# A fast causal convolution on one core: three x loads move from the set-up into the blocks of the loop

## The chip, the cores and the metric

The kernel runs on 1 core of one Trainium2 chip. The metric is device microseconds of one execution; the median of three runs is given, and for profiled executions the span from the first to the last instruction. Engines are called PE (TensorE matmul), PEld (its weight load), DVE (VectorE), ACT (ScalarE), POOL (GpSimd) and SP (SyncE).

## The reference

x has shape 8 x 4096 x 512, the kernel 8 x 512 x 512, both float32. Each output row is a sum over eight taps of an earlier row times a 512 x 512 matrix; rows ahead of the sequence's start are zero.

```python
for k in range(K):                       # K = 8
    shifted = x if k == 0 else zeros in front, x[:, :-k, :]
    out += np.matmul(shifted, kernel[k])
```

## The kernel before, in words

**Tiling.** Each of the 8 sequences is cut into 16 pieces of 256 rows, which gives 128 pieces, one for each partition. Row t then means row t of all 128 pieces: a 128 x 512 matrix. The first four rows are computed directly in the set-up, tap by tap (`direct`). The other 252 are computed in 21 blocks (0 to 20) of 12 rows, block m from row t = 4 + 12 m.

**The fast algorithm.** A block isn't computed as 12 x 8 products of a row and a tap's matrix, but by a scheme that forms sums and differences of rows (on DVE) and of tap matrices (in the set-up, `wsum` and `plus`) and so needs 36 products. Each product is four matmuls of 128x128 by 128x512 (`product`, L123), added up in PSUM. A block has four nodes: PL, MI, H1, H0, in this order, numbered from 1 on: node 4m+1 is block m's PL, node 4m+3 its H1, node 4m+4 its H0. In each node DVE makes `z`, `s`, `A` and `F` (sums of transposed rows), PE multiplies them (`a1`, `a0`, `u`, `v0`, `v1`, `l00` to `l11`), ACT copies partial sums from one PSUM bank to others (the seeds `s0`, `s1`, and `dt`, a copy into the tile DT), DVE subtracts (`d0`, `d1`), and the results are combined in y tiles of float32 and stored (`e0`, `e1`, `ga`, `gb`, `ya0`). LO and HI are a node's two halves. PSUM is three pairs of banks for results (`pp0` to `pp2`) that the nodes take in turn, and a fourth for the `a` products.

**y tiles.** There are five buffers (L45), taken in turn, for cc[LO], cc[HI], dd[LO], dd[HI], yy[LO] and yy[HI] of each block. Whoever writes a new tile has to wait until the store of the tile that had its buffer five tiles ago has landed. In block 0, the H1 node's `e1` (L269) writes yy[HI] into the buffer whose last tile was cc[LO], stored by `middle` (L295). In the loop, the same `e1` writes into the buffer of the block's own cc[LO]. That tile is finished by POOL in two halves, `ga0` and `gb0` (L300), and then stored.

**How x gets in.** Except for the first rows, x takes two steps. `load_x(t)` (L106) issues a DMA from POOL's queue that reads rows t to t+3 as float32, casts them to bfloat16 and writes them to a DRAM tile xd. Each xd tile has a buffer of its own. `transpose_x(t)` (L116) issues a DMA transpose on SP's queue from xd to XR, a ring of 20 transposed rows in SBUF. The stores go on SP's queue, too. The loads are the profile's queue q0 (software_dynamic); SP's transposes and stores are q1 (hardware_dynamic). A POOL DMA also waits for the landing of the one eight before it.

**What sets the order.** The schedule is written out by hand. The set-up is a list of calls (L430 to L646), and `go` and `do` keep a record of what has been done. The loop (L653) then goes through `ORDER` (L387) for each block: token `name.i` in block m acts on node 4m+i+1. Tokens that the set-up did already are skipped. Each engine takes its instructions in this order and waits for semaphores where its data need it. The loads of the loop are the tokens r0, r1, r2 (`rows_ahead`, L395): r_j of a node loads rows n.t + 36 + 4j onwards, where n.t is the first row of the node's block, and `behind` (L111) makes POOL wait for the last DVE instruction that stands before it in the list. `ga`, `gb` and `ya0` are put behind DVE in the same way. Block 0 runs no r tokens (L656).

- Set-up: ten loads without `behind` (rows 12 to 48), then `do("r0", 7)` and `do("r1", 7)` after H0's s (L600, L601), and `do("r2", 7)` (L638). Node 7 is block 1's H1, so these are rows 52, 56 and 60.
- Loop, block m from 1 on: r0.6, r1.6, r2.6, which is node 4m+7, the next block's H1: rows 12m+52, 12m+56, 12m+60. The last block that loads anything is block 16. On POOL's queue the order of a block is ga0, r0, gb0, r1, r2, ya0, gb1, ga1.
- Block m transposes rows 12m+16 (x12.0), 12m+24 (x20.1) and, near its end, 12m+32 (x16.4).

Of the kernel before, what the change touches and what calls it, by code (L numbers as in the profile page):

```python
# [14 lines left out]
def kernel(  # L15
# [366 lines left out]
    def s_rows(n, a, b):  # L382
# [2 lines left out]
    nodes = [None] + [Node(1 + 4 * k + i, HEAD + STEP * k, a) for k in range(NB)  # L385
                      for i, a in enumerate((PL, MI, H1, H0))]
    ORDER = """  # L387
        d1.1 l01.1 l00.1 s.2 a0.2 x12.0 u.2 l10.1 e1.0 s0.2 e0.1 s1.2 l11.1 z.3 F0.2 A.3 v0.2 F1.2 ga0.2
        v1.2 x20.1 dt.2 a1.3 d0.2 r0.6 l01.2 e1.1 l00.2 a0.3 s.3 gb0.2 d1.2 u.3 e0.2 l10.2 E0.2 z.4 F0.3
        r1.6 A.4 l11.2 s1.3 r2.6 F1.3 s0.3 v0.3 v1.3 ya0.2 dt.3 d0.3 a1.4 l01.3 e1.2 l00.3 s.4 gb1.2 a0.4  # L390
        d1.3 e0.3 u.4 l11.3 z.5 s0.4 F0.4 s1.4 dt.4 A.5 ga1.2 v0.4 v1.4 l10.3 d0.4 a1.5 d1.4 l00.4 l01.4
        a0.5 u.5 e0.4 F1.4 e1.3 s.5 s0.5 l10.4 dt.5 s1.5 z.6 A.6 x16.4 l11.4 F0.5 v0.5 v1.5 a1.6 d0.5 F1.5
    """.split()

# [25 lines left out]
    done = set()  # L420

    def do(name, k):
        if k < len(nodes) and (name, k) not in done:
            done.add((name, k))
            ACTS[name](nodes[k])

    def go(k, name):
        do("a1" if name == "b1" else name, k + AHEAD.get(name, 0))
# [168 lines left out]
    go(2, "l11")  # L597
    go(2, "z")
    go(3, "s")
    do("r0", 7)  # L600
    do("r1", 7)  # L601
    go(2, "A")
    go(3, "l01")
    go(3, "l10")
# [30 lines left out]
    go(4, "s1")  # L635
    go(4, "z")
    go(4, "A")
    do("r2", 7)  # L638
    go(4, "g1")
    go(4, "s0")  # L640
    go(4, "v0")
# [3 lines left out]
    go(4, "a1")  # L645
    go(4, "d1")  # L646

    done |= {("r0", 3), ("r1", 3), ("r2", 3)}
    done |= {(name, k) for name in ("ga0", "gb0", "ga1", "gb1", "x12", "x16", "x20")
             for k in (1, 2, 3, 4)}  # L650
    done |= {(name, k) for name in ("F0", "F1", "dt", "v0", "v1", "d0", "d1") for k in LEAF}
# [39 lines left out]
```

## Time and profile before

| | |
|---|---|
| median of 3 runs | 723.8 us (722.1 to 723.96) |
| profiled execution, its own time | 723.72 us |
| its span | 721.9 us |
| PE busy | 696.8 us (97%) |
| DVE busy | 684.3 us (95%) |
| mean granted TensorE clock | 0.998 |
| q0, the loads | 13728 packets, 32.4% of 16 DMA engines' span |
| q1, transposes and stores | 145456 packets, 45.3% |

How to read the profile. A timeline row is: start in us from the span's start, duration in us, engine, line, operation, out<-in, shapes, how many were merged, and in brackets how long the engine was idle before it and what ended that. A row of waits is: who waited, for whom, us in total, how many times, the longest in us. A row of DMA queues is: queue, kind, packets, MB, and the time of the packets as a share of 16 engines' time in the window. A row of DMA issues is: what was moved, the issuing queue, how many, KB each, and the median time in us from the issue to the landing. An "a1" copy, a seed and a DT copy are ACT's L196, L212 or L214, and L218. Matmul rows are named by what the matmul reads: F, Z, S, or w, where the tile w4 holds the early nodes' s and A.

The early part of the span, up to some 65 us, loads the tap matrices, makes their sums and computes the first four rows. Blocks 0 and 1 overlap with its end; from about 108 us POOL's first `ga0` marks block 1, and a block takes about 31 us.

### The profile page before, as it was taken

What the parts mean: (1) busy time and instruction counts of PE and PEld (TensorE: products, weight loads), DVE (VectorE), ACT (ScalarE), POOL (GpSimd) and SP (SyncE); (2) the same over time, 40 slices, a digit from 0 to 9 for tenths busy, and PEclk for the clock granted to TensorE, in tenths of its full rate; (3) what the DMA queues carried; (4) which work ended last, traced back from release to release, by engine and by line L of the source; (5) the groups of instructions that cost most, each with busy time, mean ns of one, the idle gap of its engine ahead of it and who ended that gap; (6) DMA issues with size and microseconds to landing.
All of it is one profiled execution on the core that took longest, in us unless ns stands there. A gap on an engine that the chain in (4) does not pass through costs nothing.

```text
span 721.9 us, 8973 instructions
## 1 busy us (share of the span) xinstructions
PE 696.8 (97%) x3205; PEld 315.1 (44%) x3270; DVE 684.3 (95%) x767; ACT 287.7 (40%) x448; POOL 168.0 (23%) x180
## 2 busy tenths in 40 slices
PE   7989899999999999999999999999999999999995
PEld 3444334444444444444444444444444444444442
DVE  2899799999999999999999999999999999999994
ACT  3043243544434353343434335244343534444341
POOL 4210004122131312213131230412213041221212
PEclk9999999999999999999999999999999999999999
DMA  9999879888877978877797887878688795465414
GB/s 197 210 212 219 204 152 216 186 234 167 237 152 232 230 178 220 168 225 153 227 240 168 223 167 223 195 202 244 153 233 160 216 208 168 174 118 188 160 61 174
DMA packets 159372, 138.87 MB, mean 192 GB/s; under 512 B 130144, under 2 KB 134240, under 8 KB 159200
## 3 DMA queue, kind: packets, MB, share of 16 engines
q1 hardware_dynamic: 145456, 99.89, 45.3%
q0 software_dynamic: 13728, 38.15, 32.4%
q8 instruction: 25, 0.41, 0.2%
q10 hardware_dynamic: 144, 0.26, 0.1%
q14 instruction: 19, 0.16, 0.1%
HBM read 77.33 MB, written 99.09 MB: 244 GB/s over the span
## 4 chain that ended last, share of the span: by engine, by line
PE 73%; DVE 14%; issue 3%; DMA 2%; POOL 1%; ACT 0%; POOLq 0%; DVEq 0%
PE pp L125 73%; DVE Z L84 5%; DMA out_dram<-y 2%; DVE y L87 2%; DVE S L84 2%; DVE F L84 1%; DVE y L84 1%; DVE w L84 1%; POOL y L300 1%; DVE pp L84 1%; DVE pp L87 1%; POOLq L686 0%; POOL xd L93 0%; ACT y L255 0%; ACT pp L212 0%
## 5 line engine op out<-in xcount | busy, mean ns | idle before, releaser
L125 PE MATMUL pp<-w,F 128*128 128x512 bf16 x1284 | 310.2, 379 | 2.9 <-DVE pp L84 1.0
L125 PE MATMUL pp<-w,Z 128*128 128x512 bf16 x941 | 231.9, 379 | 3.7 <-DVE Z L84 2.6
L300 POOL TENSOR_TENSOR y<-y 128x512 f32<-128x512 f32 x80 | 101.6, 1270 | 410.2 <-DVE F L84 283.7
L125 PEld LDWEIGHTS <-F 128*128 128x128 bf16 x1312 | 128.3, 98 | 157.4 <-issue 3.4
L125 PE MATMUL pp<-w,S 128*128 128x512 bf16 x659 | 157.7, 379 | 0.7
L84 DVE TENSOR_TENSOR Z<-XR 128x2048 bf16<-128x2048 bf16 (+3 forms) x109 | 154.8, 1438 | 2.4
L125 PEld LDWEIGHTS <-Z 128*128 128x128 bf16 x960 | 92.2, 98 | 119.6 <-DVE Z L84 11.2
L196 ACT COPY pp<-pp 128x512 f32<-128x512 f32 x82 | 46.7, 570 | 222.8 <-PE pp L125 222.8
L84 DVE TENSOR_TENSOR S<-Z 128x2560 bf16<-128x2560 bf16 (+1 forms) x81 | 114.7, 1416 | 0.0
L84 DVE TENSOR_TENSOR F<-S 128x1024 bf16<-128x1024 bf16 x160 | 111.4, 696 | 1.9 <-PE pp L125 1.9
L125 PEld LDWEIGHTS <-S 128*128 128x128 bf16 x672 | 65.7, 98 | 79.4
L212 ACT COPY pp<-pp 128x512 f32<-128x512 f32 (+1 forms) x84 | 48.9, 582 | 74.9 <-PE pp L125 74.9
L93 POOL DMA_DIRECT2D xd<-in_x_dram x61 | 32.2, 528 | 109.3 <-DVE F L84 45.8
L87 DVE SCALAR_TENSOR_TENSOR pp<-pp,DT 128x512 f32<-128x512 f32 x82 | 56.8, 692 | 0.5 <-PE pp L125 0.5
L84 DVE TENSOR_TENSOR pp<-DT,pp 128x512 f32<-128x512 f32 x82 | 56.6, 690 | 0.3 <-PE pp L125 0.2
L214 ACT ACTIVATE pp<-pp 128x512 f32<-128x512 f32 (+1 forms) x84 | 50.2, 597 | 16.5 <-PE pp L125 8.1
L84 DVE TENSOR_TENSOR Z<-Z 128x1024 bf16<-128x1024 bf16 x78 | 53.5, 686 | 0.7
L87 DVE SCALAR_TENSOR_TENSOR y<-pp,y 128x1024 f32<-128x1024 f32 x42 | 51.2, 1218 | 0.5 <-PE pp L125 0.5
L218 ACT COPY DT<-pp 128x512 f32<-128x512 f32 x82 | 49.1, 598 | 3.9 <-PE pp L125 3.9
L257 ACT COPY y<-pp 128x1024 f32<-128x1024 f32 x40 | 40.6, 1016 | 23.7 <-PE pp L125 22.5
L87 DVE SCALAR_TENSOR_TENSOR y<-y,pp 128x1024 f32<-128x1024 f32 (+1 forms) x41 | 48.4, 1183 | 1.7 <-POOL y L300 1.4
L84 DVE TENSOR_TENSOR y<-pp,y 128x1024 f32<-128x1024 f32 (+1 forms) x42 | 40.4, 962 | 6.8 <-DMA out_dram<-y 6.8
(35 smaller groups left out, 251.1 us busy)
## 6 DMA issues: line engine op xcount, KB each, us to landing
out_dram<-y SPq DMA_DIRECT2D x127, 512.0 KB, 4.4
xd<-in_x_dram POOLq DMA_DIRECT2D x61, 512.0 KB, 5.7
w<-in_kernel_dram POOLq DMA_DIRECT2D x8, 512.0 KB, 16.5
w<-in_x_dram SPq DMA_DIRECT2D x1, 1024.0 KB, 4.8
w<-in_x_dram POOLq DMA_DIRECT2D x2, 512.0 KB, 13.7
XR<-xd SPq DMA_TRANSPOSE x61, 4.7
w<-in_x_dram POOLq DMA_DIRECT2D x2, 256.0 KB, 17.3
w<-in_x_dram POOLq DMA_DIRECT2D x1, 384.0 KB, 20.2
```

What stands on the lines that cost most here:

```text
L84: last["dve"] = nc.vector.tensor_tensor(out=o, in0=a, in1=b, op=op)
L87: last["dve"] = nc.vector.scalar_tensor_tensor(out=o, in0=a, scalar=by, in1=b, op0=MUL, op1=op)
L93: return nc.gpsimd.dma_start(out=o, in_=src)
L125: nc.tensor.matmul(bank, lhsT=comp[:, c * P:(c + 1) * P], rhs=w[:, c, :], start=start and c == 0, stop=c == DC - 1, skip_group_check=True)
L196: nc.scalar.copy(out=n.q[:, 0], in_=n.q[:, 1])
L212: nc.scalar.copy(out=o, in_=q)
L214: nc.scalar.mul(out=o, in_=q, mul=-1.0)
L218: nc.scalar.copy(out=DT, in_=n.q[:, 0])
L257: nc.scalar.copy(out=cc[b_], in_=p)
L300: behind(nc.gpsimd.tensor_tensor(out=cc[b_][:, j], in0=cc[b_][:, j], in1=dd[b_][:, j], op=ADD))
```

## The change

The two calls for r0 and r1 and the one for r2 leave the set-up, and the line that recorded r0 to r2 of node 3 as done goes with them. In `ORDER`, r0.6, r1.6 and r2.6 become r0.2, r1.2 and r2.2: block m now loads rows 12m+40, 12m+44 and 12m+48. Rows 52, 56 and 60 are thus loaded by block 1, and block 17 is the last one that loads. r0 and r1 keep their places in the list; r2 moves from ahead of F1.3 to behind ya0.2. On POOL's queue a block becomes ga0, r0, gb0, r1, ya0, r2, gb1, ga1. The tokens v0.2, s.3, u.3 and A.5 also move by one to three places past tokens of other engines. The number of loads, 61, is the same.

```diff
     ORDER = """
-        d1.1 l01.1 l00.1 s.2 a0.2 x12.0 u.2 l10.1 e1.0 s0.2 e0.1 s1.2 l11.1 z.3 F0.2 A.3 v0.2 F1.2 ga0.2
-        v1.2 x20.1 dt.2 a1.3 d0.2 r0.6 l01.2 e1.1 l00.2 a0.3 s.3 gb0.2 d1.2 u.3 e0.2 l10.2 E0.2 z.4 F0.3
-        r1.6 A.4 l11.2 s1.3 r2.6 F1.3 s0.3 v0.3 v1.3 ya0.2 dt.3 d0.3 a1.4 l01.3 e1.2 l00.3 s.4 gb1.2 a0.4
-        d1.3 e0.3 u.4 l11.3 z.5 s0.4 F0.4 s1.4 dt.4 A.5 ga1.2 v0.4 v1.4 l10.3 d0.4 a1.5 d1.4 l00.4 l01.4
+        d1.1 l01.1 l00.1 s.2 a0.2 x12.0 u.2 l10.1 e1.0 s0.2 e0.1 s1.2 l11.1 v0.2 z.3 F0.2 A.3 F1.2 ga0.2
+        v1.2 x20.1 dt.2 a1.3 d0.2 r0.2 l01.2 e1.1 l00.2 s.3 a0.3 u.3 gb0.2 d1.2 e0.2 l10.2 E0.2 z.4 F0.3
+        r1.2 A.4 l11.2 s1.3 F1.3 s0.3 v0.3 v1.3 ya0.2 r2.2 dt.3 d0.3 a1.4 l01.3 e1.2 l00.3 s.4 gb1.2 a0.4
+        d1.3 e0.3 u.4 l11.3 z.5 s0.4 F0.4 A.5 s1.4 dt.4 ga1.2 v0.4 v1.4 l10.3 d0.4 a1.5 d1.4 l00.4 l01.4
         a0.5 u.5 e0.4 F1.4 e1.3 s.5 s0.5 l10.4 dt.5 s1.5 z.6 A.6 x16.4 l11.4 F0.5 v0.5 v1.5 a1.6 d0.5 F1.5
...
-    do("r0", 7)
-    do("r1", 7)
     go(2, "A")
...
-    do("r2", 7)
     go(4, "g1")
...
-    done |= {("r0", 3), ("r1", 3), ("r2", 3)}
```

## The prediction

> **What bounds the kernel now.** I read, in this order: the busy times of the engines, the chain of work that ended last, the waits of VectorE (DVE) stage by stage, and then the timelines of the one stage in which DVE waits. Page first, busy times and chain:
>
> ```profile
> PE 696.8 (97%) x3205; PEld 315.1 (44%) x3270; DVE 684.3 (95%) x767; ACT 287.7 (40%) x448; POOL 168.0 (23%) x180
> ...
> PE 73%; DVE 14%; issue 3%; DMA 2%; POOL 1%; ACT 0%; POOLq 0%; DVEq 0%
> ```
>
> Two engines are nearly full, so little can be won: all that TensorE (PE) loses. From 125 us to 700 us PE is held up in two places only, near 308 and 558 us (1.1 and 0.7 us beyond its regular gap of 0.05 us every 10.8 us). Most of the rest lies between 85 and 125 us: 4.4 us of gaps. There the chain runs through DVE, and DVE's only wait there stands ahead of it. DVE's waits from 72 to 90 us, then its timeline:
>
> ```profile
> DVE y L84 <- DMA out_dram<-y: 4.6, 1, 4.6
> ```
> ```profile
> 76.82 0.68 DVE L84 TENSOR_TENSOR w<-Z 128x1024 bf16<-128x1024 bf16 x1
> 82.14 1.23 DVE L84 TENSOR_TENSOR y<-pp,y 128x1024 f32<-128x1024 f32 x1 [4.64 <-DMA out_dram<-y]
> ...
> 85.41 1.22 DVE L84 TENSOR_TENSOR y<-y,pp 128x1024 f32<-128x1024 f32 x1
> ...
> 90.41 0.69 DVE L84 TENSOR_TENSOR pp<-DT,pp 128x512 f32<-128x512 f32 x1
> ```
>
> DVE is free at 77.50 and starts `e1` of block 0's H1 node at 82.14. It writes a y buffer whose earlier content, cc[LO], was stored at 73.79; that store landed at 82.02, after 8.23 us. Why so late? POOL's timeline and the DMA traffic from 74.4 to 78.2 us, then the issues from 83.4 to 86.6 us:
>
> ```profile
> 71.19 1.02 POOL L93 DMA_DIRECT2D xd<-in_x_dram  x2 [28.42 <-DVE S L84]
> ```
> ```profile
> q0 software_dynamic: 154, 0.57, 105.1%
> ...
> q1 hardware_dynamic: 1, 0.00, 0.3%
> ```
> ```profile
> out_dram<-y SPq DMA_DIRECT2D x1, 512.0 KB, 3.2
> ```
>
> The two loads at 71.19 are set-up's r0 and r1 (rows 52 and 56). While their packets (q0) fill the engines, one single packet of q1, the store's queue, moves in 3.8 us. A store of the same size with no load beside it lands in 3.2 us.
>
> **The change part by part.** The built program's order on PE, DVE, ACT and SP, and the kinds of events they wait for, are the same before and after; only POOL's queue differs. So the moved tokens v0.2, s.3, u.3 and A.5 cost nothing by themselves: each passes only tokens of other engines.
>
> *Loads of rows 52 and 56 leave set-up.* The store issued at 73.79 then has idle DMA engines: the last transpose lands at 71.29. Its landing is the unknown. Bounds: 2.6 us (block 17, no load anywhere near), 3.2 us (the row above), 5.5 us (the slowest store of cc[LO] in the loop, at 299.0, with a load ahead of it). I take 3.2 us, the nearest in time and place: landing 77.0, before DVE is free at 77.50. The wait goes altogether; with 5.5 us it would be 79.3 and 1.8 us of the wait stay.
>
> What is late next? PE's and ACT's timelines:
>
> ```profile
> 83.81 1.89 PE L125 MATMUL pp<-w,S 128*128 128x512 bf16 x8
> 87.77 2.75 PE L125 MATMUL pp<-w,w 128*128 128x512 bf16 x11 [2.08 <-ACT pp L212]
> 91.15 1.89 PE L125 MATMUL pp<-w,F 128*128 128x512 bf16 x8 [0.63 <-DVE pp L84]
> ...
> 98.92 1.04 PE L125 MATMUL pp<-w,Z 128*128 128x512 bf16 x4 [0.71 <-DVE Z L84]
> ```
> ```profile
> 84.01 0.59 ACT L218 COPY DT<-pp 128x512 f32<-128x512 f32 x1 [2.83 <-PE pp L125]
> 86.66 0.58 ACT L214 ACTIVATE pp<-pp 128x512 f32<-128x512 f32 x1 [2.06 <-DVE y L84]
> 87.15 0.57 ACT L212 COPY pp<-pp 128x512 f32<-128x512 f32 x1
> ```
>
> 1. DVE from 77.50 has 8.27 us of work in a row (82.14 to 90.41) up to `d0` of node 5, block 1's PL node: it could start that at 85.77, 4.64 earlier.
> 2. `e0` of node 4, 3.27 us after `e1`, ends near 82.0 and no longer holds ACT's seed s1 (the 2.06 us). ACT now waits for PE alone: DT copy at 84.01 as before, s1 at 84.5, s0 at 85.0 (spacing 0.5), done at 85.6.
> 3. PE ends its eight S matmuls' slots at 83.81 + 8 x 0.216 = 85.54 (0.216 from starts: 80.35 to 82.08 for eight) and starts `v0` of node 5 at 85.65, not 87.77.
> 4. `d0` needs those four matmuls: 85.65 + 1.03 = 86.68. It starts at 86.7, not 85.77. So DVE keeps 90.41 - 86.7 = **3.7 us** of the 4.64; 0.9 us turns into a wait for PE.
> 5. From there DVE runs back to back as before. A of node 7 (98.18) comes at 94.5, and the matmuls at 98.92 can start at 95.2. PE has 44 matmuls to do from 85.65: 9.5 us, to 95.15. Both arrive together, 3.7 us early. After that the stage is DVE's as it was, moved by 3.7 us as a whole, and from 125 us PE's.
>
> With the 5.5 us landing, DVE is 4.64 - 1.8 = 2.8 us early and the gain is 2.8. It can't be over 4.64 either: that is the whole wait.
>
> *Load of row 60 leaves set-up (89.65).* It delays the stores at 90.52 and 92.25 (6.8 and 6.3 us to landing), but DVE has no wait from 90 to 200 us, and ACT none for a DMA but one of 1.1 us in the whole loop. Gain 0.
>
> *Every block loads rows one block sooner than it used to need them, and block 17 loads too.* In block terms the traffic of blocks 1 to 16 is the same: three loads each, at the same places. Only the lead shrinks. The shortest is row 56's kind: r1 of block 1 is issued at 114.88, lands after 4.75 us, and is transposed at 161.40; 41.8 us remain against 10.0 us for the slowest loop load. Cost 0. Block 17 gets three loads it did not have; blocks 2 to 16 with such loads show PE busy 19.89 of 20 us, as blocks 17 to 19 do without. Cost 0, at worst one more wait like those near 308 and 558 us: 1.1.
>
> The Trainium skill speaks against this part: "DMA: Bandwidth & Descriptors", Rules for kernel authors, says to issue a DMA early and wait late. By it a later load could only lose; by the 41.8 us above it loses nothing here, and early issue is just what puts the loads ahead of the store.
>
> *The third load (r2) moves behind F1 and behind ya0 on POOL.*
>
> ```profile
> 114.88 1.11 POOL L93 DMA_DIRECT2D xd<-in_x_dram  x2 [2.79 <-DVE F L84]
> 116.00 1.28 POOL L292 TENSOR_TENSOR y<-y 128x512 f32<-128x512 f32 x1
> 118.99 1.27 POOL L300 TENSOR_TENSOR y<-y 128x512 f32<-128x512 f32 x1 [1.71 <-DVE S L84]
> ```
>
> ya0 waits for DVE's F1, done at 115.79, so it starts at most 0.2 us sooner. r2 is then issued at 117.2 to 117.8 instead of 115.4 to 116.0. Behind it on POOL stands gb1, which waits for DVE until 118.99: 1.2 us of cover; without it, up to 0.55 us on gb1 and its store. The stores of yy[LO] and yy[HI] (117.31 and 117.73, now 8.2 and 9.0 us to landing, behind r1 and r2 as the cc[LO] store was in set-up) should get ahead of r2 and land some 4 us sooner. ACT's next y copy, which reuses yy[LO]'s buffer, starts at 126.69 when PE lets it, 1.2 us after that landing: nobody waited, so gain 0; bounds 0 and the 1.1 us of ACT's one odd wait.
>
> The same page of the skill, Queues, rings and completion order, says a DMA engine takes turns between its queues packet by packet. Then r2's place among the stores would hardly matter; the q0 and q1 rows above (154 packets against 1) show no such turns. By either, this part is worth 0 in the sum.
>
> **Sum.** The profiled execution took 723.72 us (span 721.9 plus 1.8 around it): 723.72 - 3.7 = **720.0 us**. The median of the runs is 723.8, practically the same.
>
> **The rivals.**
> - *More: the two loop waits go too.* Near 308 and 558 us DVE waits 1.33 and 0.85 us for a cc[LO] store that landed in 5.5 and 5.1 us, not 3.2 to 3.7. If a changed traffic spares it, 1.1 + 0.7 us more: 718.2. Against: r2 is issued after that landing or at the tail of it, and r0 and r1 stay. Chance 0.10.
> - *Less, or not what it says: the store is late without the loads, or another wait takes over.* For: the store shares SP's queue and buffers with others, and step 4 shows PE already near. Against: 3.2 us beside transposes. Gain 0 to 2.1: about 722.5. Chance 0.16.
> - *Slower: r2 later than its gap.* r2's traffic ends later, pushes the transposes that start at 130.37, these push r0 (140.38) and so the cc[LO] store (143.18). That landing has 0.7 to 1.0 us of slack before DVE's e1 (147.39). Price: 0.7 us of PE, as near 558 us, in each of 17 blocks, 12 us: 732. It decides once r2's delay passes on more than 1.0 us; r2 is 1.8 us later. Against: DMA work from 116 to 129.5 us is unbroken, so reordering it should not end it later. Chance 0.06.
>
> **How the numbers follow.** Forecast: 0.68, 719.2 to 721.0. A measurement tells 0.3% (2.2 us) from no change, so faster means under 721.6. Forecast and "more" are faster, 0.78; I move 0.03 of it to "same" for landings near 5.5 us with run spread (722.1 to 723.96 before). Faster 0.75, same 0.18, slower 0.07. The range takes in "more" at the bottom and most of "less" at the top: 717.9 to 722.6.
>
> **What would show it.** Right: no DVE wait on out_dram near 77 us; the cc[LO] store near 73.8 lands in about 3 us; a DVE wait on PE of about 0.9 us ahead of `d0`; PE's 2.08 us gap gone; POOL's first loop tensor (108.02) near 104.3, and every later block 3.7 us sooner. Wrong: the store still lands after 77.5; ACT or PE waits that are new between 77 and 95 us; DVE waits on out_dram in many blocks of the loop.

## The result and the profile after

The changed kernel takes **720.55 us** (median of 6 runs, 719.45 to 721.05), the one before 723.44 us in the runs beside it (722.1 to 724.04): a ratio of 0.996, 95% interval 0.9947 to 0.9973, which is a gain of 2.9 us with an interval of 2.0 to 3.8. 720.0 us was forecast. The profiled execution took 720.38 us, its span is 718.6 us. The busy times and the chain on its page:

```profile
PE 699.3 (97%) x3270; PEld 314.9 (44%) x3270; DVE 684.3 (95%) x767; ACT 287.6 (40%) x448; POOL 167.6 (23%) x180
...
PE 79%; DVE 10%; issue 2%; DMA 1%; POOL 1%; ACT 0%; POOLq 0%; DVEq 0%
```

DVE's and the stores' part of the chain has shrunk (14% to 10%, 2% to 1%), and PE's has grown: the end is set by matmuls over more of the span. PE's busy times can't be compared: 65 of the 3270 matmuls have no record in the profile before. The place of the old wait, in DVE's timeline, and then the DMA traffic from 73.9 to 76.7 us with the issues in that window:

```profile
77.02 0.68 DVE L84 TENSOR_TENSOR w<-Z 128x1024 bf16<-128x1024 bf16 x1
77.62 1.22 DVE L84 TENSOR_TENSOR y<-pp,y 128x1024 f32<-128x1024 f32 x1
...
80.88 1.21 DVE L84 TENSOR_TENSOR y<-y,pp 128x1024 f32<-128x1024 f32 x1
...
86.94 0.69 DVE L84 TENSOR_TENSOR pp<-DT,pp 128x512 f32<-128x512 f32 x1 [0.98 <-PE pp L125]
```
```profile
q1 hardware_dynamic: 144, 0.52, 46.1%
...
out_dram<-y SPq DMA_DIRECT2D x1, 512.0 KB, 2.7
```

The store of cc[LO], issued at 74.00, has the DMA engines to itself and lands after 2.7 us instead of 8.23. `e1` follows A without a gap, and the only wait that is left is new: 0.98 us for PE, ahead of `d0` of node 5. PE's timeline of the same stage:

```profile
84.01 1.89 PE L125 MATMUL pp<-w,S 128*128 128x512 bf16 x8
85.81 2.75 PE L125 MATMUL pp<-w,w 128*128 128x512 bf16 x12
88.40 1.89 PE L125 MATMUL pp<-w,F 128*128 128x512 bf16 x8
...
95.46 1.04 PE L125 MATMUL pp<-w,Z 128*128 128x512 bf16 x4
```

The gaps of 2.08, 0.63 and 0.71 us are gone. POOL's queue in block 1 shows r2 (113.67) behind ya0 (112.46):

```profile
111.42 0.54 POOL L93 DMA_DIRECT2D xd<-in_x_dram  x1 [2.78 <-DVE F L84]
112.46 1.28 POOL L292 TENSOR_TENSOR y<-y 128x512 f32<-128x512 f32 x1 [0.50 <-DVE F L84]
113.67 0.54 POOL L93 DMA_DIRECT2D xd<-in_x_dram  x1
115.54 1.27 POOL L300 TENSOR_TENSOR y<-y 128x512 f32<-128x512 f32 x1 [1.32 <-DVE S L84]
```

DVE's waits from 100 to 600 us still hold the two of the loop, in blocks 7 and 15:

```profile
DVE y L84 <- DMA out_dram<-y: 2.0, 2, 1.5
```

To compare single executions, which begin up to 1.6 us apart in the load of the first matrices, I cut the span at two events that every kernel here has: PE's gap of 1.2 us near 48 us, and the first ga0 in the loop. The four rows, of before and then of changed, PE and POOL each:

```profile
49.18 1.02 PE L125 MATMUL pp<-w,w 128*128 128x512 bf16 x4 [1.22 <-ACT pp L214]
108.02 1.27 POOL L300 TENSOR_TENSOR y<-y 128x512 f32<-128x512 f32 x1 [17.85 <-DVE F L84]
```
```profile
49.38 0.81 PE L125 MATMUL pp<-w,w 128*128 128x512 bf16 x3 [1.21 <-ACT pp L214]
104.56 1.27 POOL L300 TENSOR_TENSOR y<-y 128x512 f32<-128x512 f32 x1 [61.58 <-DVE F L84]
```

Between them the kernel before takes 58.84 us, the changed one 55.18: 3.66 us less. From ga0 to the end they take 613.93 and 614.06 us. The whole difference is made before the loop. What follows the last ga0 takes 19.6 or 20.0 us, and both values occur with and without the change, so a difference of 0.4 us from ga0 to the end says nothing.

### The profile page after: what moved, and what is told of

Its sections match the earlier page's. It is cut to its first block, busy times and chain, and to the rows that moved or that the text cites. A ratio compares the mean times of both kernels' runs of the same rounds, so it can differ in the third digit from the quotient of the medians.

```text
span 718.6 us, 9022 instructions
## 1 busy us (share of the span) xinstructions
PE 699.3 (97%) x3270; PEld 314.9 (44%) x3270; DVE 684.3 (95%) x767; ACT 287.6 (40%) x448; POOL 167.6 (23%) x180
## 4 chain that ended last, share of the span: by engine, by line
PE 79%; DVE 10%; issue 2%; DMA 1%; POOL 1%; ACT 0%; POOLq 0%; DVEq 0%
PE pp L125 79%; DVE Z L84 4%; DVE S L84 1%; DVE y L87 1%; DMA out_dram<-y 1%; DVE F L84 1%; DVE w L84 1%; POOL y L300 1%; DVE y L84 1%; DVE pp L84 0%; DVE pp L87 0%; POOLq L682 0%; POOL xd L93 0%; ACT y L255 0%; ACT pp L212 0%
## 5 line engine op out<-in xcount | busy, mean ns | idle before, releaser
L259 ACT ACTIVATE y<-y 128x1024 f32<-128x1024 f32 x40 | 42.3, 1057 | 2.5 <-DMA out_dram<-y 0.4
```

Source lines behind the costliest of these rows:

```text
L259: nc.scalar.mul(out=dd[b_], in_=cc[b_], mul=-0.5)
```

## The experiments

Theory A is the prediction's: block 0's cc[LO] store stands behind two set-up loads, and DVE waits for it. Theory B: the gain comes from r2's new place in the loop. Theory C: it comes from less load traffic in the set-up as such. All ratios are to the kernel before, beside which each was run. There it took 723.06 us beside setup_only, r2_only, setup_loads_late and three_loads, 722.82 beside one_load and r0_behind_gb0, and 723.19 beside loop_r0_only and three_together, so ratios and not times compare kernels of different groups. The last three columns are of one profiled execution each.

| kernel | time, us | ratio (95%) | DVE's wait for that store, us | gap to ga0, us | ga0 to end, us |
|---|---|---|---|---|---|
| before | 723.44 | | 4.64 | 58.84 | 613.93 |
| changed | 720.55 | 0.9960 (0.9947 to 0.9973) | 0 | 55.18 | 614.06 |
| setup_only | 719.72 | 0.9952 (0.9939 to 0.9965) | 0 | 55.17 | 614.51 |
| r2_only | 722.68 | 0.9995 (0.9985 to 1.0005) | 4.28 | 58.46 | 613.62 |
| setup_loads_late | 719.70 | 0.9958 (0.9943 to 0.9973) | 0 | 55.18 | 614.79 |
| three_loads | 723.64 | 1.0012 (1.0000 to 1.0025) | 5.48 | 59.66 | 613.79 |
| one_load | 720.44 | 0.9971 (0.9959 to 0.9984) | 3.04 | 57.22 | 614.14 |
| r0_behind_gb0 | 716.89 | 0.9925 (0.9910 to 0.9940) | 0 | 55.17 | 611.83 |
| loop_r0_only | 721.12 | 0.9974 (0.9963 to 0.9986) | 4.71 | 58.89 | 611.80 |
| three_together | 717.42 | 0.9923 (0.9908 to 0.9938) | 0 | 55.17 | 612.41 |

**setup_only.** The changed kernel with r2 at its old place in the loop.

```diff
-        r1.2 A.4 l11.2 s1.3 F1.3 s0.3 v0.3 v1.3 ya0.2 r2.2 dt.3 ...
+        r1.2 A.4 l11.2 s1.3 r2.2 F1.3 s0.3 v0.3 v1.3 ya0.2 dt.3 ...
```

> The change without its other half: r0 to r2 leave the set-up, but r2 keeps its old place in the loop, ahead of F1.3 and ya0. Theory A (the cc[LO] store of block 0 stands behind two set-up loads, and DVE waits 4.6 us for it): the whole gain stays, 720.0 to 721.0 us, no DVE wait on out_dram near 77 us, ratio 0.996. Theory B (the gain comes from the loop, where r2 no longer stands ahead of the yy stores): the gain is gone, 723 us, ratio 1.00; the yy[LO] stores of the loop land after 8 us as before under both.

Measured: 719.72 us. The stretch to ga0 is that of the changed kernel to 0.01 us, while the yy[LO] stores of blocks 1 to 17 take 7.7 to 8.8 us to land. Theory B is out as the source of the gain. DVE's waits from 72 to 100 us:

```profile
DVE pp L84 <- PE pp L125: 1.0, 1, 1.0
```

**r2_only.** The kernel before with r2 behind ya0.

```diff
-        r1.6 A.4 l11.2 s1.3 r2.6 F1.3 s0.3 v0.3 v1.3 ya0.2 dt.3 ...
+        r1.6 A.4 l11.2 s1.3 F1.3 s0.3 v0.3 v1.3 ya0.2 r2.6 dt.3 ...
```

> The other half alone: the set-up keeps its three loads, r2 of each block stands behind ya0. Theory A: 723.4 us, ratio 1.000 within 0.002, DVE's wait of 4.6 us near 77 us stays; the yy[LO] stores land after 4 to 5 us and not 8, and nobody profits. Theory B: 720.5 us, ratio 0.996.

Measured: 722.68 us, ratio 0.9995. The yy[LO] stores land after 4.3 to 7.7 us and not 7.6 to 9.2; nobody profits. The wait stays, in the waits from 72 to 100 us:

```profile
DVE y L84 <- DMA out_dram<-y: 4.3, 1, 4.3
```

**setup_loads_late.** The kernel before with r0 and r1 of the set-up behind the H1 node's e1. Nothing leaves the set-up.

```diff
-    do("r0", 7)
-    do("r1", 7)
     go(2, "A")
...
     go(3, "e1")
+    do("r0", 7)
+    do("r1", 7)
```

> The kernel before with all its set-up loads, but r0 and r1 of the set-up stand behind the H1 node's e1 of block 0, so they are issued at about 78.8 us and not at 71.2. Theory A: only their place ahead of the store matters, so the full gain is there although nothing leaves the set-up: 720.0 to 721.0 us. Theory C (it is the amount of load traffic in the set-up, or the room on POOL's queue): no gain, 723.4 us.

Measured: 719.70 us, ratio 0.9958, and a stretch of 55.18 us. The same two loads, 7.5 us later, cost nothing there, although the stores and the transpose behind them and the third load now take 11 to 16 us to land. Only ACT waits for such a store, 0.59 and 0.19 us near 97 and 98 us, and that doesn't lengthen the stretch to ga0. Theory C falls. That the rows are loaded a block later isn't needed for the gain, either.

**three_loads.** The kernel before with the set-up's r2 beside r0 and r1.

```diff
     do("r1", 7)
+    do("r2", 7)
     go(2, "A")
...
-    do("r2", 7)
     go(4, "g1")
```

> The kernel before with the set-up's r2 moved up beside r0 and r1, three loads ahead of the store. Theory A: one more load of about 4 us of all DMA engines' time is ahead of the store; it lands near 86 us, DVE waits about 8.5 us and not 4.6, and the time is about 727 us (ratio 1.005). Theory C: the same amount of traffic, 723.4 us. If DMA engines took turns between the two queues packet by packet, the store would hardly be later for a third load that queues behind the second: 723 to 724 us.

Measured: 723.64 us, ratio 1.0012, where I had expected 727; 723 to 724 had been put down for DMA engines that take turns. The sign is that of theory A (the interval begins at 1.0000), the size isn't. DVE waits for 5.5 us, not 8.5; the store lands at 81.76, ahead of the third load (83.66). DVE's waits from 72 to 100 us, then the DMA queues from 76.5 to 82 us and from 80.2 to 81.7 us:

```profile
DVE y L84 <- DMA out_dram<-y: 5.5, 1, 5.5
```
```profile
q0 software_dynamic: 203, 0.76, 70.8%
q1 hardware_dynamic: 187, 0.70, 33.6%
```
```profile
q0 software_dynamic: 57, 0.23, 76.5%
q1 hardware_dynamic: 55, 0.16, 30.0%
```

Here loads and stores do move side by side, 203 packets against 187. The 203 hold the end of the second load, which landed at 80.14, and the 187 the first packets of the next store; in the shorter window only the third load is left on q0, and it is 57 against 55. The counts fit a store that stands behind the two loads that were first and shares the engines with the third; the profile doesn't say which engine moved a packet. The Trainium skill ("DMA: Bandwidth & Descriptors", Queues, rings and completion order) has the DMA engines take turns between their queues. My prediction found no such turns in the window beside two loads (154 packets against 1). Both are seen. The page's turn is a whole packet of several descriptors, and no run here shows how many of the profile's packets make one, so a conflict with the page isn't shown, nor what ended the time without turns after two loads (256 data packets of 4 KB).

**one_load.** The kernel before with only r0 ahead of the store; r1 stands beside r2.

```diff
     do("r0", 7)
-    do("r1", 7)
     go(2, "A")
...
+    do("r1", 7)
     do("r2", 7)
     go(4, "g1")
```

> The kernel before with only r0 (row 52) at its place in the set-up ahead of the cc[LO] store; r1 stands beside r2, near 89 us. Theory A: the single load lands near 76.7 us, the store some 0.8 us behind it, near 77.5 us, just when DVE is free: DVE waits 0 to 0.3 us, 720.0 to 721.0 us. Theory C (the traffic): nothing left, 723.4 us. A share in proportion to the loads ahead of the store would give 722 us.

Measured: 720.44 us in the median, inside what was expected, but partly by luck: the kernel before took 722.82 us beside it and not 723.4. The ratio, 0.9971, lies nearer to the share in proportion (722 of 723.4 us, 0.998) than to the full gain (0.9952 to 0.9960), and its interval reaches both. The profiled execution shows another way there. DVE's timeline:

```profile
79.19 1.23 DVE L84 TENSOR_TENSOR y<-pp,y 128x1024 f32<-128x1024 f32 x1 [3.04 <-PE pp L125]
```

DVE waits 3.04 us, not 0 to 0.3. The row names PE, but the matmuls of that tile had long been done: the store landed at 79.07. It lands 6.6 us after its issue. The load ahead of it took 8.2 us itself, one of its packets 1.9 us, and an instruction fetch began at 76.02; the store landed 3.05 us after that, as the late stores of the loop do (see r0_behind_gb0). So this execution shows one load with such a packet and such a fetch on top: 2.05 us over no load (57.22 against 55.17), where two loads cost 3.66. What one load alone costs stays open, and theory A's size for it was too small in this execution.

The rows of the table now form one line. Take 54.20 us (58.84 - 4.64) and add the wait: 59.68 for 5.48, 58.48 for 4.28, 57.24 for 3.04, against 59.66, 58.46 and 57.22 measured. With no wait that would be 54.20; measured is 55.18, and the 0.98 us between is DVE's new wait for PE.

**r0_behind_gb0.** The changed kernel with r0 of each block behind gb0, and so behind the block's own cc[LO] store.

```diff
-        v1.2 x20.1 dt.2 a1.3 d0.2 r0.2 l01.2 e1.1 l00.2 s.3 a0.3 u.3 gb0.2 d1.2 ...
+        v1.2 x20.1 dt.2 a1.3 d0.2 l01.2 e1.1 l00.2 s.3 a0.3 u.3 gb0.2 r0.2 d1.2 ...
```

> The changed kernel with r0 of each block issued behind gb0 and so behind the block's own cc[LO] store, not between ga0 and gb0. Theory A carried on: the two waits left in the loop (DVE 1.5 and 0.5 us near 301 and 551 us) are the same mechanism, a store behind a load with an instruction fetch on top; the store now lands after 2.6 to 3.6 us in every block, both waits go, and PE wins back 1.2 + 0.6 us: 718.8 us. Rival D: the fetch alone makes these waits, and the place of r0 doesn't matter: 720.5 us. The risk is that the yy stores, now behind r0 and r1, hold up ACT's next y copy: then 721 us or more with ACT waits on out_dram.

Measured: **716.89 us**, ratio 0.9925: faster than both kernels (the changed one's interval is 0.9947 to 0.9973). From ga0 on it takes 611.83 us instead of 614.06, 2.2 us less where 1.8 had been expected; most of the rest of the surprise lies ahead of PE's 1.2 us gap, which comes 1.5 us sooner in this execution than in the changed kernel's, and the kernel before was faster in this group, too. The cc[LO] stores of blocks 1 to 17 land after 3.5 to 4.0 us, not 2.6 to 3.6. The risk was real and small: ACT waits for stores five times in the loop, 3.2 us in all, and PE has no gap from it. DVE's waits from 100 to 600 us:

```profile
DVE pp L84 <- PE pp L125: 0.2, 1, 0.2
```

Both waits on stores are gone. Why just blocks 7 and 15 had them, the traces show. About once in 28 us the profile has an instruction fetch, one packet of 16 KB, mostly 0.9 to 1.4 us long. In each of the seven traces that have r0 ahead of the store, the only cc[LO] stores over 4.2 us to landing are those of blocks 7 and 15, and they are also the only ones with a fetch 1.4 to 2.8 us after their issue; they land 3.0 to 3.2 us after that fetch begins. With r0 behind gb0, the fetch of those two blocks runs 0.5 to 1.1 us ahead of the store's issue, in three traces of three. From the changed kernel, 297.9 to 299.2 us (the store is issued at 295.5), then from r0_behind_gb0, 292.6 to 294.0 us (the store at 294.0):

```profile
q1 hardware_dynamic: 34, 0.08, 16.5%
q8 instruction: 1, 0.02, 4.6%
```
```profile
q8 instruction: 1, 0.02, 4.4%
```

In the first the fetch (q8) runs among the store's packets, in the second alone and ahead of it. It seems that the fetch, too, stands behind r0's packets: in the 14 cases it begins 0.5 to 0.8 us before r0 has landed. That isn't shown, since the profile doesn't name a packet's engine.

Rival D, the fetch alone, falls only so far: the place of r0 decides whether a fetch comes late. A late fetch puts off a store without any load, too. In each of the ten traces one begins 0.3 to 0.8 us after the issue of a store between 681 and 689 us, 60 us or more after the last load landed, and that store lands after 3.3 to 3.9 us instead of 2.6, which is 3.0 to 3.4 us after the fetch began. From the kernel before, the issue at 683.8 without a fetch, then the one at 688.3 with a fetch 0.43 us behind it:

```profile
out_dram<-y SPq DMA_DIRECT2D x1, 512.0 KB, 2.6
```
```profile
out_dram<-y SPq DMA_DIRECT2D x1, 512.0 KB, 3.5
```

With r0 ahead, the fetch of blocks 7 and 15 comes 1.4 to 2.8 us after the issue, and the store lands after 4.5 to 5.9 us. `e1` comes some 4.2 us after the store's issue (143.18 and 147.39 in block 2 before), which neither the load alone (3.1 to 4.1 us) nor a fetch alone, as far as seen, takes up. So the two waits come from both together.

**loop_r0_only.** The kernel before with r0 behind gb0, set-up loads and all.

```diff
-        v1.2 x20.1 dt.2 a1.3 d0.2 r0.6 l01.2 e1.1 l00.2 a0.3 s.3 gb0.2 d1.2 ...
+        v1.2 x20.1 dt.2 a1.3 d0.2 l01.2 e1.1 l00.2 a0.3 s.3 gb0.2 r0.6 d1.2 ...
```

> The kernel before, set-up loads and all, with only r0 of each block moved behind gb0 and so behind the block's own cc[LO] store. If the two kinds of wait are independent, the 4.3 to 4.7 us wait near 77 us stays and the stretch from PE's 1.2 us gap near 48 us to the first ga0 stays at 58.5 to 58.9 us, while the loop's waits on out_dram are gone and the rest, from the first ga0 to the end, is 611.8 us and not 613.6 to 614.8: 2 us less than before, 720.6 to 721.0 us, ratio 0.997. If r0 behind gb0 worked only together with the change, there is no gain: 722.8 us.

Measured: 721.12 us, ratio 0.9974; 58.89 us to ga0 and 611.80 from there, as expected. DVE's waits from 72 to 100 us; from 100 to 600 us it has none:

```profile
DVE y L84 <- DMA out_dram<-y: 4.7, 1, 4.7
```

The two waits are independent: 0.9952 (setup_only) x 0.9974 = 0.9926, and both together gave 0.9925.

**three_together.** r0_behind_gb0 with r2 at its old place, so that r0, r1 and r2 all stand ahead of the yy stores.

```diff
-        r1.2 A.4 l11.2 s1.3 F1.3 s0.3 v0.3 v1.3 ya0.2 r2.2 dt.3 ...
+        r1.2 A.4 l11.2 s1.3 r2.2 F1.3 s0.3 v0.3 v1.3 ya0.2 dt.3 ...
```

> The changed kernel with r0 behind gb0, but r2 back at its old place ahead of ya0: now r0, r1 and r2 all stand ahead of the yy stores. It asks whether r2's new place is worth something when there is more load ahead. If the yy[LO] store now lands 2 us or more later than the 8.3 us that it takes with r2 behind ya0, ACT's next y copy, which starts about 14 us after that store's issue less 5, waits in most blocks, its seeds come late and PE loses: 719 to 725 us. If r2 doesn't matter here either: 716.9 us, with ACT's waits on out_dram a few us in all, as with r2 behind ya0.

Measured: 717.42 us, ratio 0.9923, no difference from r0_behind_gb0 that the intervals could tell. The yy[LO] stores land after 8.3 to 9.9 us (8.2 to 9.5 with r2 behind ya0). ACT's waits from 100 to 720 us:

```profile
ACT y L257 <- DMA out_dram<-y: 4.6, 3, 1.8
ACT y L259 <- DMA out_dram<-y: 0.6, 1, 0.6
```

ACT begins to wait, three times for its y copy (near 434, 465 and 528 us), but PE has no gap over its regular 0.05 us there. Of the 0.58 us that this execution takes longer from ga0 on, 0.36 lie behind the last ga0. r2's place comes nearer to mattering here and still doesn't.

## Why the prediction was right

- *The wait and its cause.* Right. Without loads ahead of it the store lands in 2.7 us (3.2 was taken) and the 4.64 us go. setup_loads_late shows that the place of the loads does it, not their number. The fetch isn't the cause here: before, one began at 74.57, 0.78 us after the store's issue, and the store landed 7.4 us later, not 3.0.
- *What is late next (steps 1 to 5).* Right nearly to the digit. Predicted: 0.9 us of the wait turns into a wait for PE, and 3.7 us remain. Measured in the profiled executions: 0.98 and 3.66 us; the medians alone (2.9 us, interval 2.0 to 3.8) couldn't tell the 3.7 from the 2.8 of a 5.5 us landing. Everything in this execution is 0.2 us later than before already at PE's 1.2 us gap, hence 86.94 for `d0` and not 86.7, and 104.56 for the first ga0 and not 104.3.
- *The load of row 60, the shorter lead, block 17's loads.* Right: 0 each. From ga0 to the end the kernels differ by 0.13 us. Two readings behind it are off and change nothing: the slowest load of the loop took 10.5 us to land, not 10.0, and ACT's wait of 1.1 us is put down to "remote" by its row and not to a DMA.
- *r2 behind ya0.* Right at 0 by itself (r2_only, 0.9995), and the yy[LO] stores do land some 4 us sooner, 4.2 us instead of 8.2 in block 1. The yy[HI] stores don't, against the forecast: 8.4 us instead of 9.0 in block 1. They are issued 0.5 us behind r2 (114.19 against 113.67), the yy[LO] store 0.1 us behind it. The reading that q0 and q1 show no turns was too broad: three_loads shows turns with a third load.
- *The two loop waits* stayed, as the forecast had it: 1.5 and 0.5 us in place of 1.33 and 0.85. In the profile before they end at 304.6 and 554.8 us, and PE's gaps at 307.9 to 312.2 and 562.4, rather than near 308 and 558.
- *The rivals.* "More" was possible, but by another edit, r0 behind gb0. "Less" falls with the landing of 2.7 us, "slower" with the loop's time. The chances don't add up as told: 0.03 moved to "same" gives 0.19 and 0.06 where 0.18 and 0.07 stand.

The 0.55 us between 720.0 and 720.55 is within the spread of the runs. The forecast stood on one execution's own time, 0.28 us over the later median of before.

## What to carry to other kernels

Where two engines are 95% full, look for the one wait that stands ahead of a stretch in which the other engine follows. Then ask what was issued to the DMA engines just before the transfer that is waited for: here moving two loads behind a store, with no byte less to move, was worth 0.4%, and one load behind another store 0.3% more. And follow the freed engine to the next thing it needs: 0.98 of the 4.64 us came back as a wait for PE.

## What the runs showed of the hardware

- A store of 512 KB takes 2.6 to 2.7 us to land on idle DMA engines, 8.2 us when it is issued 2 us after two loads of 512 KB each, and up to 11.6 us behind three loads and a transpose (setup_loads_late).
- A third load didn't push the store back in full: once the first two had landed, loads and stores moved side by side (57 packets to 55 in 1.5 us).
- An instruction fetch of 16 KB that began after a store's issue put off its landing to 3.0 to 3.4 us after the fetch began: 4.5 to 5.9 us behind a load (3.1 to 4.1 without the fetch), 3.3 to 3.9 us with no load near (2.6 without).
